# Raising the scheduler's priority of the attention row pairs in a hybrid FoX and mLSTM layer

## The chip, the cores and the metric

The kernel runs on one core of one Trainium2 chip. Its time is the device time of one execution in microseconds (us). The core has five engines that each work off their own queue of instructions in order: TensorE (PE, matrix products), VectorE (DVE), ScalarE (ACT), GpSimd (POOL) and SyncE (SP, which here issues DMAs). An instruction that needs something from another engine waits at the head of its queue, and what stands behind it waits too.

## The reference

One layer of a hybrid decoder: x is 2048 tokens of width 1024, in float32.

```
h  = rmsnorm(x);  z = h @ w_in                       # q, k, v, gates
fox = softmax(q k^T * d^-0.5 + c_t - c_s, causal) v  # 8 heads of 64, c = cumsum(log_sigmoid(f))
ml  = chunkwise matrix memory, 4 heads of 128
x  = x + concat(headnorm(fox), headnorm(ml) * sigmoid(o)) @ w_out
x  = x + relu(rmsnorm(x) @ w_up)^2 @ w_down
x  = x + sigmoid(rmsnorm(x) @ w_pg) * (p @ w_ple);  return rmsnorm(x)
```

The change touches only the order in which the `fox` line is worked.

## The kernel before

The program has three stretches. Up to about 560 us it makes the mLSTM half and the first projections. From about 560 to 1322 us it works the FoX attention. After that come the output projection, the MLP and the gate.

Attention goes head by head, and in a head by row pairs: `ROWS` pairs the sixteen blocks of 128 query rows as (15), (14, 0), (13, 1) to (8, 6), (7), so that nine steps have nearly the same work. A pair's scores lie side by side in *units*, tiles of 1024 columns; a head has 17 units, all heads 136. A name such as `s1_8_0_4` says head 1, the pair that begins with row block 8, the pair's first row block (0), key blocks from 4 on; `sp1_8_1`, `ph1_8_1` and `pt1_8_1` are unit 1 of that pair. Below, "unit 13,1 of head 1" means `..1_13_1`.

For each pair `fox_rows` records this chain:

- PE makes scores in chunks of at most 512 columns (L798, L800, for the diagonal also L803) into PSUM tiles `s`, of which there are three (SB).
- DVE adds the bias, keeps the running maximum and writes the unit's tile `sp` (L806); four `sp` tiles exist (SPB). Then DVE makes the exponent's offset `nb` (L818).
- ACT takes the exponential in place (L821), then casts the unit to float16 in a tile `ph` (L826); four `ph` tiles exist (PHB), and the norms borrow them too (`psq`, `po`).
- POOL, for each eighth unit DVE, subtracts the cast from the exact value for a second float16 half (L828).
- SP issues a DMA that transposes both halves into a tile `pt` (L830); three exist (PTB).

`fox_av` then multiplies the transposed unit with the values on PE (L846, L847, L849), three small matmuls a key block, and DVE copies the result out (L852). `fox_post` norms a group of finished rows and sends it on.

`fox_attn` calls these: a head begins with the loads of its two bias tiles (L890) and their scaling (L893); for each pair it records `fox_rows`, then a share of filler work (`fill`: the next heads' projections `zfq`, `zv`, `zfk`, the embedding product `pp`, the mLSTM output product `om`), and the value products of the pair that was recorded LAG = 3 pairs earlier.

What is recorded is not yet the order of the engines. The framework simulates a list scheduler: every instruction gets a priority by its place in the recording, and each engine takes, among the instructions whose inputs and buffers it holds to be ready by then, the one with the best priority. The result is a fixed queue for each engine; waits on semaphores are put in, and on the chip the order can't change any more. A tile taken again (the fifth `sp`, the fourth `pt`) waits there for the last use of the one that had its place.

Of the kernel before, what the change touches and what calls it, by code (L numbers as in the profile page):

```python
# [54 lines left out]
def hybrid_layer(ctx, tc, x, p, w_in, b_fox_f, b_mlstm_i, b_mlstm_f, w_conv, g_mix,  # L55
# [725 lines left out]
    def fox_rows(fl, fpp, h, rows, bias, fs, qkl):  # L781


        Qt, Kt, KL = qkl
        tag = f"{h}_{rows[0]}"
        nu = (sum(rows) + len(rows) + 7) // 8
        st = [fl.tile([P, 1024], F32, tag="sp", name=f"sp{tag}_{u}", bufs=SPB)
              for u in range(nu)]
        at = 0
        for r, i in enumerate(rows):  # L790
            qs = slice(i * P, (i + 1) * P)
            mx, kb, parts = None, 0, []
            while kb <= i:
                u, o = divmod(at + kb, 8)
                n = min(4, 8 - o, 8 - kb % 8, i + 1 - kb)
                ps = fpp.tile([P, 512], F32, tag="s", name=f"s{tag}_{r}_{kb}", bufs=SB)
                ks = slice(kb * P, (kb + n) * P)
                PE.matmul(ps[:, 0:n * P], lhsT=Qt[:, qs], rhs=Kt[:, ks], start=True, stop=False)  # L798
                diag = kb + n > i
                PE.matmul(ps[:, 0:n * P], lhsT=Qt[:, qs], rhs=KL[:, ks], start=False,  # L800
                          stop=not diag)
                if diag:
                    PE.matmul(ps[:, (n - 1) * P:n * P], lhsT=identb, rhs=fneg, start=False,  # L803
                              stop=True)
                m = fl.tile([P, 1], F32, tag="mx", name=f"mx{tag}_{r}_{kb}", bufs=8)
                V.tensor_tensor_reduce(out=st[u][:, o * P:(o + n) * P], in0=ps[:, 0:n * P],  # L806
                                       in1=bias[kb // 8][:, kb % 8 * P:(kb % 8 + n) * P],
                                       scale=1.0, scalar=-3.0e38 if mx is None else mx,
                                       op0=ALU.add, op1=ALU.max, accum_out=m)
                mx = m  # L810
                if parts and parts[-1][0] == u:
                    parts[-1][2] = o + n
                else:
                    parts.append([u, o, o + n])
                kb += n
            at += i + 1
            nb = fl.tile([P, 1], F32, tag="nb", name=f"nb{tag}_{r}", bufs=8)
            V.tensor_scalar(nb, mx, fs[:, 1:2], LN_P, op0=ALU.mult, op1=ALU.add)  # L818
            for u, o0, o1 in parts:
                sl_ = st[u][:, o0 * P:o1 * P]  # L820
                A.activation(sl_, sl_, AF.Exp, bias=nb, scale=fs[:, 0:1])  # L821
        pts = []
        for u in range(nu):
            ph = fl.tile([P, 2048], F16, tag="ph", name=f"ph{tag}_{u}", bufs=PHB)
            cnt[0] += 1
            A.copy(ph[:, 0:1024], st[u])  # L826
            eng = V if cnt[0] % DM == 3 else T
            eng.tensor_sub(ph[:, 1024:2048], st[u], ph[:, 0:1024])  # L828
            pt = fl.tile([P, 16, P], F16, tag="pt", name=f"pt{tag}_{u}", bufs=PTB)
            SP.dma_start_transpose(out=pt, in_=ph)  # L830
            pts.append(pt)
        return pts
# [23 lines left out]
    def drain(n):  # L856
        while sum(e[0] for e in avq) > n or (avq and not avq[0][0]):
            e = avq.pop(0)
            if e[0]:
                fox_av(*e[1:])  # L860
            else:
                posts.append([PD_, *e[1:]])

    def mix_load(lo, hi):

        for g in GD:
            if lo:
                mt_ = tp.tile([P, 2, KT, GT], F16, tag="T", name=f"mix{g}")
                mg[g] = mt_[:, 0], mt_[:, 1]
            gs = slice(g * GT, (g + 1) * GT)  # L870
            for a in range(2):
                SP.dma_start(out=mg[g][a][:, lo:hi, :],
                             in_=mixd[lo:hi, :, a, gs].rearrange("k p s -> p k s"))
                yield

    def late(all_=False):
        for e in posts:
            e[0] -= 1
        while posts and (all_ or posts[0][0] <= 0):
            fox_post(*posts.pop(0)[1:])  # L880

    def fox_attn(fl, fpp, j, z, fill):
        fs, iv, vt, qkls = z
        ogs = {}
        for hh in range(2):
            h = 2 * j + hh
            bias = {}
            for sg in (1, 0):
                b = fl.tile([P, 1024], F32, tag="bias", name=f"bias{h}_{sg}", bufs=2)
                SP.dma_start(out=b.rearrange("p (t s) -> p t s", s=P),  # L890
                             in_=crow[h * NT + 8 * sg:h * NT + 8 * sg + 8, :]
                             .partition_broadcast(P))
                V.tensor_scalar(b, b, fs[:, 2:3], None, op0=ALU.mult)  # L893
                bias[sg] = b
            for k, rows in enumerate(ROWS):
                pts = fox_rows(fl, fpp, h, rows, bias, fs, qkls[hh])
                for i in rows:
                    if hh == 0 and i // 4 not in ogs:
                        ogs[i // 4] = fl.tile([P, 4, 2, FD + 1], F32, tag="og",
                                              name=f"og{j}_{i // 4}", bufs=4)  # L900
                fill(sum(rows) + len(rows) + RC)
                avq.append((1, fl, fpp, h, rows, pts, vt, ogs))
                if hh == 1 and k in DONE:
                    g = DONE[k]
                    avq.append((0, fl, j, g, ogs[g], iv))
                drain(LAG)
                late()
                if h == FH - 2 and k == LK:
                    loads.append(mix_load(0, NP - 1))
                if loads:  # L910
                    next(loads[0], None)
        if j == NP - 1:
            for _ in loads[0]:
                pass
            for k in range(LAG - 1, -1, -1):
                fill(FE)
                drain(k)
                late()
            fill(1e9)
            late(all_=True)  # L920
# [36 lines left out]
    with phase("fl", 2) as fl, phase("fps", 2, PSUM) as fpp:  # L957
        def filler(parts, total):

            parts = iter(parts)  # L960
            st = [0.0, next(parts, None)]

            def fill(n):
                flush()
                st[0] += n * total / (272.0 + 18 * RC)
                while st[1] is not None and st[0] >= st[1]:
                    st[0] -= st[1]
                    st[1] = next(parts, None)
            return fill

        for j in range(NP):
            nxt = []
            if j < NP - 1:
                if j == 0:
                    plsp[0] = fl.tile([P, S], F16, name="plsp", bufs=1)
                    ple_w()
                fill = filler(pair_parts(j, nxt), TOT)
            else:
                for _ in mix_load(NP, KT):
                    pass  # L980
                fill = filler(late_parts(), FT)
            fox_attn(fl, fpp, j, box[0], fill)
            fill(1e9)
            second_keys()
            box = nxt
# [207 lines left out]
```

## Time and profile before

| | |
|---|---|
| median of three runs | 2950.56 us (2950.12 to 2952.53) |
| the profiled execution | 2954.44 us, of it 2952.7 us span |
| mean granted clock of TensorE | 0.968 of full speed |
| PE busy over the span | 2698.4 us (91%) |
| DVE, ACT, POOL busy | 1621.7, 1008.3, 698.7 us |
| attention, 560 to 1322 us | PE busy 608.1 of 762 us |
| after attention, 1322 to 2952.7 us | PE busy 1591.0 of 1630.7 us |

How to read it: time is lost where PE stands idle or is granted less than full clock. An engine's idle time has a releaser, the event that ended it; the views of waits add these up by the pair of lines. Busy shares over the whole span hide that nearly all of PE's idle time of the second half lies in attention.

### The profile page before, as it was taken

How to read it: one execution, taken by the hardware profiler on the slowest of the kernel's cores; microseconds unless marked ns; L12 is line 12 of the kernel's file. 1: busy time of each engine (PE TensorE's matmuls, PEld its weight loads, DVE VectorE, ACT ScalarE, POOL GpSimd, SP SyncE). 2: the span in 40 equal slices, each digit the busy share in tenths (PEclk: the TensorE clock that was granted, in tenths of full speed). 3: DMA queues.
4: the chain of work that ended last, by engine and by line, in shares of the span. 5: the costliest groups of instructions: out<-in, count | busy, mean ns of one | idle time of the engine just before them, and what ended most of it. 6: DMA issues, size and time to landing. Idle time of an engine off the chain costs nothing. (4 is left out here: it accounts for less than half of the span.)

```text
span 2952.7 us, 45034 instructions
## 1 busy us (share of the span) xinstructions
PE 2698.4 (91%) x18229; PEld 1507.1 (51%) x18229; DVE 1621.7 (55%) x3633; ACT 1008.3 (34%) x1686; POOL 698.7 (24%) x435
## 2 busy tenths in 40 slices
PE   4998999888878788788999999999999999999997
PEld 2756767555454554343344444444444444444686
DVE  6464654766757657556654444444444444445636
ACT  6244444465555555553411111111111111113532
POOL 1011110244343444343122111111212111111132
PEclk9999999989899989999999999999999999999999
DMA  9212220387686879996700000000000000002623
GB/s 243 45 44 59 58 47 20 94 167 137 139 166 133 165 169 219 196 205 222 148 29 29 29 29 16 28 15 29 29 29 29 29 29 16 28 15 43 143 69 136
DMA packets 535265, 256.36 MB, mean 87 GB/s; under 512 B 432784, under 2 KB 502672, under 8 KB 535056
## 3 DMA queue, kind: packets, MB, share of 16 engines
q1 hardware_dynamic: 525296, 236.66, 35.0%
q10 hardware_dynamic: 9760, 16.82, 1.8%
q8 instruction: 142, 2.33, 0.3%
q14 instruction: 67, 0.55, 0.1%
HBM read 113.88 MB, written 32.60 MB: 50 GB/s over the span
## 5 line engine op out<-in xcount | busy, mean ns | idle before, releaser
L1054 PE MATMUL d<-wd_hl,hid 128*128 128x512 f16 x3072 | 678.2, 380 | 8.4 <-DVE x L1059 8.2
L1036 PE MATMUL h<-y1t,wu_hl 128*128 128x512 f16 x3072 | 673.5, 379 | 0.5 <-issue 0.5
L1054 PEld LDWEIGHTS <-hid 128*128 128x128 f16 x3072 | 301.3, 98 | 375.0 <-issue 15.8
L1036 PEld LDWEIGHTS <-wu_hl 128*128 128x128 f16 x3072 | 300.5, 98 | 363.2 <-ACT y1y L200 1.0
L1059 DVE SCALAR_TENSOR_TENSOR x<-d,fac,x 128x512 f32<-128x512 f32 x512 | 373.8, 747 | 132.2 <-PE d L1054 131.8
L1044 POOL TENSOR_TENSOR hid<-r,hid 128x512 f16<-128x512 f32 x128 | 174.5, 1364 | 765.2 <-ACT hid L1043 659.1
L1042 DVE SCALAR_TENSOR_TENSOR r<-h,r 128x512 f32<-128x512 f32 x128 | 88.3, 690 | 458.2 <-ACT r L1040 458.1
L1040 ACT ACTIVATE r<-h 128x512 f32<-128x512 f32 x128 | 75.9, 594 | 766.8 <-PE h L1036 763.3
L828 POOL TENSOR_TENSOR ph<-sp,ph 128x1024 f16<-128x1024 f32 x119 | 255.9, 2164 | 283.3 <-ACT ph L826 219.3
L271 PEld LDWEIGHTS <-yt 128*128 128x128 f16 x3072 | 251.6, 101 | 40.1 <-issue 13.7
L260 PE MATMUL zqk<-yt,wqk_hl 128*128 128x512 f16 x768 | 188.7, 393 | 27.9 <-DMA yt<-yy 27.9
L821 ACT ACTIVATE sp<-sp,nb,fs 128x1024 f32<-128x1024 f32 (+3 forms) x192 | 177.9, 982 | 85.2 <-DVE nb L818 60.5
L798 PE MATMUL s<-K,Q 128*128 128x512 f16 (+3 forms) x320 | 117.9, 369 | 79.4 <-DVE mx L806 76.4
L846 PE MATMUL av<-vt,pt 128*128 128x65 f16 x1088 | 121.9, 199 | 67.3 <-DMA pt<-ph 55.6
L271 PE MATMUL zvo<-wvo_hl,yt 128*128 128x256 f16 x1536 | 175.0, 275 | 4.1 <-ACT wvo_hl L155 2.8
L1007 PE MATMUL pg<-wpg_hl,y2t 128*128 128x256 f16 x1536 | 171.0, 275 | 4.7 <-DVE x L1059 4.0
L1007 PEld LDWEIGHTS <-y2t 128*128 128x128 f16 x1536 | 151.6, 99 | 24.1 <-issue 5.1
L826 ACT CAST ph<-sp 128x1024 f16<-128x1024 f32 x136 | 137.8, 1038 | 67.9 <-DMA pt<-ph 62.6
L846 PEld LDWEIGHTS <-pt 128*128 128x128 f16 x1088 | 105.3, 100 | 75.1 <-DMA pt<-ph 67.8
L806 DVE CUSTOM_DVE_ANT_0 sp<-s,bias,mx 128x512 f32<-128x512 f32 (+2 forms) x192 | 124.5, 648 | 29.4 <-POOL ph L828 14.2
L260 PEld LDWEIGHTS <-wqk_hl 128*128 128x128 f16 x768 | 77.4, 101 | 105.5 <-ACT wqk_hl L155 25.9
L641 PEld LDWEIGHTS <-mix 128*128 128x128 f16 x768 | 76.4, 102 | 101.6 <-issue 27.7
(380 smaller groups left out, 3648.2 us busy)
## 6 DMA issues: line engine op xcount, KB each, us to landing
x<-in_x_dram SPq DMA_DIRECT2D x32, 512.0 KB, 5.8
wu_st<-in_w_up_dram SPq DMA_DIRECT2D x16, 1024.0 KB
wd_st<-in_w_down_dram SPq DMA_DIRECT2D x16, 1024.0 KB, 4.9
bias<-crow SPq DMA_DIRECT2D x16, 512.0 KB, 5.9
pled<-fox_st ACTq DMA_DIRECT2D x32, 256.0 KB, 2.8
wod<-spare ACTq DMA_DIRECT2D x32, 256.0 KB, 5.0
wos<-wod SPq DMA_DIRECT2D x32, 256.0 KB, 3.9
emb<-pled SPq DMA_DIRECT2D x32, 256.0 KB, 3.0
```

Of the source, the lines that this page charges most:

```text
L260: PE.matmul(ps, lhsT=hl[:, a, kt, m * P:(m + 1) * P], rhs=yT[g][b][:, kt, :], start=i == 0, stop=i == 3 * KT - 1)
L271: PE.matmul(ps[:, 0:n], lhsT=yT[g][b][:, kt, o:o + P], rhs=hl[:, a, kt, 0:n], start=i == 0, stop=i == 3 * KT - 1)
L806: V.tensor_tensor_reduce(out=st[u][:, o * P:(o + n) * P], in0=ps[:, 0:n * P], in1=bias[kb // 8][:, kb % 8 * P:(kb % 8 + n) * P], scale=1.0 ...
L821: A.activation(sl_, sl_, AF.Exp, bias=nb, scale=fs[:, 0:1])
L826: A.copy(ph[:, 0:1024], st[u])
L828: eng.tensor_sub(ph[:, 1024:2048], st[u], ph[:, 0:1024])
L846: PE.matmul(ar, lhsT=pt[:, o, :], rhs=vs[:, 0:65], start=kb == 0, stop=False)
L1007: PE.matmul(ps, lhsT=aT[t // 4][ya][:, kt, o:o + P], rhs=hl[:, wa, kt, :], start=i == 0, stop=i == 3 * KT - 1)
L1036: PE.matmul(ps, lhsT=wu[:, a, kt, m * P:(m + 1) * P], rhs=y1T[g][b][:, kt, :], start=i == 0, stop=i == 3 * KT - 1)
L1044: T.tensor_sub(hid[:, 1, m], r2, hid[:, 0, m])
L1054: PE.matmul(ps, lhsT=hid[:, a, m, t * P:(t + 1) * P], rhs=wd[:, b, m, hf * 512:(hf + 1) * 512], start=i == 0, stop=i == 5)
L1059: V.scalar_tensor_tensor(xs, ps, fac, xs, ALU.mult, ALU.add)
```

## The change

One call is put into a block that sets the scheduler's priority.

```
             for k, rows in enumerate(ROWS):
-                pts = fox_rows(fl, fpp, h, rows, bias, fs, qkls[hh])
+                with tc.high_priority():
+                    pts = fox_rows(fl, fpp, h, rows, bias, fs, qkls[hh])
                 for i in rows:
```

Within the block every instruction that `fox_rows` records, from the score matmul to the issue of the transpose, gets a priority ahead of all that is recorded outside: projections, value products, their copies, norms, bias loads. Each block starts its count at zero again, so that the instructions of two row pairs tie: the tenth of a later pair ranks with the tenth of an earlier one, not behind the earlier pair's last. No instruction is added, removed or changed; every buffer count is as before. After the changed line the line numbers of the new kernel are greater by one.

On PE, in head 1 near the end of its nine pairs, the rows below run from the last value product of unit 13,0 to the first score chunk of pair (7). First the kernel before:

```order
L849 MATMUL av_6239<-vt0_5167,pt1_13_0_7431 128x65
...
L798 MATMUL s1_9_0_0_7956<-K_5163,Q0_5162 128x512
...
L849 MATMUL av_6239<-vt0_5167,pt1_12_1_7606 128x65
L798 LDWEIGHTS Q0_5162
L798 MATMUL s1_8_0_0_8080<-K_5163,Q0_5162 128x512
...
L849 MATMUL av_6239<-vt0_5167,pt1_11_1_7750 128x65
L798 LDWEIGHTS Q0_5162
L798 MATMUL s1_7_0_0_8203<-K_5163,Q0_5162 128x512
```

The same stretch of the changed kernel:

```order
L798 MATMUL s1_8_1_0_8100<-K_5163,Q0_5162 128x512
...
L849 MATMUL av_6239<-vt0_5167,pt1_13_0_7431 128x65
...
L798 MATMUL s1_8_1_4_8105<-K_5163,Q0_5162 128x384
...
L260 MATMUL zfk1_2_8002<-yt2_285,fox_hl_5118 128x512
L798 LDWEIGHTS Q0_5162
L798 MATMUL s1_7_0_0_8203<-K_5163,Q0_5162 128x512
...
L798 MATMUL s2_15_0_0_8365<-K_5163,Q1_5944 128x512
...
L846 MATMUL av_6239<-vt0_5167,pt1_12_0_7601 128x65
```

Before, the value products of pairs (12, 2) and (11, 3), the scores of two pairs and 48 matmuls of `zfk` lie between the first row and `s1_7_0_0`. Now it is 24 value matmuls of unit 13,1, one score chunk and 21 matmuls of `zfk1_2`, and even the next head's first scores (`s2_15_0_0`) stand ahead of the value products of pair (12, 2).

On ACT, the exponentials (L821), casts (L826) and copies of keys (L769) of head 1 around pair (9, 5), before:

```order
L821 ACTIVATE sp1_10_1_7831<-sp1_10_1_7831,nb1_10_1_7863,fs0_5299 128x640
L826 CAST ph1_10_0_7866<-sp1_10_0_7830 128x1024
L769 ACTIVATE K_5163<-zfk1_1_7878 64x512
L826 CAST ph1_10_1_7871<-sp1_10_1_7831 128x1024
L821 ACTIVATE sp1_9_0_7954<-sp1_9_0_7954,nb1_9_0_7972,fs0_5299 128x1024
L821 ACTIVATE sp1_9_1_7955<-sp1_9_1_7955,nb1_9_0_7972,fs0_5299 128x256
```

and of the changed kernel:

```order
L826 CAST ph1_10_0_7866<-sp1_10_0_7830 128x1024
L769 ACTIVATE K_5163<-zfk1_1_7878 64x512
L821 ACTIVATE sp1_9_0_7954<-sp1_9_0_7954,nb1_9_0_7972,fs0_5299 128x1024
L821 ACTIVATE sp1_9_1_7955<-sp1_9_1_7955,nb1_9_0_7972,fs0_5299 128x256
L821 ACTIVATE sp1_9_1_7955<-sp1_9_1_7955,nb1_9_1_7987,fs0_5299 128x768
L826 CAST ph1_10_1_7871<-sp1_10_1_7831 128x1024
```

The cast of unit 10,1 now stands behind the three exponentials of the next pair.

On SP, the transposes (L830) and the loads of head 2's bias (L890) at the end of head 1, before:

```order
L830 DMA_TRANSPOSE pt1_10_0_7869<-ph1_10_0_7866 128x16x128
L890 DMA bias2_1_8357<-crow_382 128x1024
L830 DMA_TRANSPOSE pt1_10_1_7874<-ph1_10_1_7871 128x16x128
...
L830 DMA_TRANSPOSE pt1_7_0_8220<-ph1_7_0_8217 128x16x128
L716 DMA fox_st_5119<-in_w_in_dram 128x8x128
L890 DMA bias2_0_8360<-crow_382 128x1024
```

and of the changed kernel:

```order
L830 DMA_TRANSPOSE pt1_11_0_7745<-ph1_11_0_7742 128x16x128
L890 DMA bias2_1_8357<-crow_382 128x1024
L890 DMA bias2_0_8360<-crow_382 128x1024
L830 DMA_TRANSPOSE pt1_11_1_7750<-ph1_11_1_7747 128x16x128
L830 DMA_TRANSPOSE pt1_10_0_7869<-ph1_10_0_7866 128x16x128
```

The second bias load (`bias2_0`), which has to wait for the last use of head 1's `bias1_0` by pair (7), moves ahead of eight transposes.

## Rows read from the trace of the kernel before

**Rows 1.** Windows by stretch, columns named in the first line; PEclk is the granted clock.

```profile
core 0: us, PE busy (x) PEld busy (x) DVE busy (x) ACT busy (x) POOL busy (x), PEclk, DMA share, GB/s
560.00:1322.00 762.00, 608.10 (x6322) 369.70 (x6321) 489.55 (x1516) 414.99 (x530) 309.00 (x159) 0.92 0.80 163
680.00:768.00 88.00, 74.09 (x754) 42.67 (x751) 65.14 (x186) 43.15 (x56) 30.65 (x17) 0.96 0.70 133
768.00:874.00 106.00, 78.10 (x976) 55.78 (x974) 63.89 (x228) 57.25 (x79) 41.43 (x23) 0.92 0.79 155
1322.00:2952.70 1630.70, 1591.04 (x8085) 792.87 (x8081) 822.11 (x1353) 350.85 (x587) 327.55 (x233) 0.99 0.19 54
```

**Rows 2.** Waits of PE, 560 to 1322 us: line, releaser, total us, times, longest.

```profile
PE s L798 <- DVE mx L806: 76.4, 43, 4.9
PE av L846 <- DMA pt<-ph: 55.6, 35, 6.6
```

**Rows 3.** Waits of DVE, 560 to 1322 us.

```profile
DVE bias L893 <- DMA bias<-crow: 31.1, 12, 6.2
DVE sp L806 <- POOL ph L828: 27.8, 19, 5.9
```

**Rows 4.** Waits of ACT, 560 to 1322 us.

```profile
ACT ph L826 <- DMA pt<-ph: 62.6, 26, 6.0
```

**Rows 5.** Waits of SP's queue, 560 to 1322 us.

```profile
SPq L830 <- PE av L849: 53.1, 23, 5.9
```

**Rows 6.** Line L830, the transposes: issue min/median/max ns; then issue to landing.

```profile
L830 SPq DMA_TRANSPOSE pt<-ph x136: 1317/2472/7229, 584.4 to 1313.0; - x136
...
DMA to landing us min/median/max: 4.3/5.2/10.1
```

**Rows 7.** Timeline, PE, head 1: start, duration, line, operation, [idle before, its releaser].

```profile
706.99 0.19 PE L849 MATMUL av<-vt,pt 128*128 128x65 f16 x1
707.70 0.20 PE L847 MATMUL av<-vt,pt 128*128 128x64 f16 x1
710.12 0.38 PE L798 MATMUL s<-K,Q 128*128 128x512 f16 x1 [0.85 <-DVE mx L806]
711.30 4.70 PE L260 MATMUL zfk<-yt,fox_hl 128*128 128x512 f16 x21
```

**Rows 8.** Timeline of the same stretch, SP's queue, ACT, POOL and DVE.

```profile
707.26 14.58 SPq L830 DMA_TRANSPOSE pt<-ph  x4
711.75 1.04 ACT L826 CAST ph<-sp 128x1024 f16<-128x1024 f32 x1 [4.58 <-DMA pt<-ph]
712.92 2.14 POOL L828 TENSOR_TENSOR ph<-sp,ph 128x1024 f16<-128x1024 f32 x1 [3.98 <-DVE mx L806]
709.98 0.08 DVE L806 DVE_READ_ACCUMULATOR2_ANT mx<- 128x1 f32 x1
710.21 0.75 DVE L806 CUSTOM_DVE_ANT_0 sp<-s,bias,mx 128x512 f32<-128x512 f32 x1
```

**Rows 9.** Timeline, PE, the first chunks that wait in heads 2, 4 and 5.

```profile
753.47 0.39 PE L798 MATMUL s<-K,Q 128*128 128x512 f16 x1 [3.16 <-DVE mx L806]
754.34 0.63 PE L798 MATMUL s<-K,Q 128*128 128x512 f16 x1
939.16 0.39 PE L798 MATMUL s<-K,Q 128*128 128x512 f16 x1 [2.59 <-DVE mx L806]
1035.14 0.58 PE L798 MATMUL s<-K,Q 128*128 128x512 f16 x1 [4.32 <-DVE mx L806]
```

**Rows 10.** Timeline, DVE and SP, the end of head 1 and start of head 2.

```profile
732.40 0.73 DVE L806 CUSTOM_DVE_ANT_0 sp<-s,bias,mx 128x512 f32<-128x512 f32 x1
744.21 0.58 SPq L890 DMA_DIRECT2D bias<-crow  x1
750.96 0.75 DVE L893 TENSOR_SCALAR bias<-bias,fs 128x1024 f32<-128x1024 f32 x1 [1.31 <-DMA bias<-crow]
```

**Rows 11.** Window of PE behind the wait at 753.47: length, busy, granted clock, DMA share.

```profile
753.00:757.00 4.00, 3.53 (x11) 0.63 0.18 64
```

## The prediction

> **What bounds the kernel now.** I read the windows by stretch first. After attention PE is busy 1591.0 of 1630.7 us, and the change moves nothing there. In attention it is busy 608.1 of 762 [rows 1], so 153.9 us of idle time are all that the change can win, and new idle time there is all that it can lose. No other engine is full: DVE, the busiest after PE, has 490 of 762.
>
> The waits of PE come second. Two pairs of lines hold most of the 154 us: a score chunk that waits until DVE has read the chunk three before it (76.4 us in 43 waits), and a value product that waits for its transposed unit (55.6 us in 35) [rows 2]. The waits of DVE, ACT and SP say what stands behind the first: DVE waits 31.1 us for bias tiles and 27.8 us, in 19 waits, for POOL to leave an `sp` tile [rows 3]; ACT's cast waits 62.6 us for the transpose that frees a `ph` tile [rows 4]; SP's transposes wait 53.1 us for the value products that free a `pt` tile [rows 5].
>
> So there is a round trip through the tiles that are taken again. Counted in units, the transpose of unit u waits for the value products of u-3, the cast for the transpose of u-4, the score pass of DVE for the subtraction of u-4, and a score chunk for the DVE pass three chunks earlier. A score chunk so waits for value products eleven units back. The timeline gives its length. In head 1 the last value matmul of unit 13,0 ends at 706.99 + 0.19 = 707.18 [rows 7]; SP goes on at 707.26; the cast starts at 711.75, released by a landing; POOL's subtraction runs from 712.92 to 715.06 [rows 8]. That is 7.9 us. A DVE pass of 0.75 us follows, and about 0.14 us from the read of the maximum at 709.98 to the matmul it releases at 710.12 [rows 7, 8]: 8.8 us. For the second unit of a pair, whose value products end 24 x 0.031 = 0.75 us later (0.031 by the 23 steps from 706.99 to 707.70 [rows 7]), but whose transpose stands behind one of 2.47 us [rows 6], it is 8.8 + 2.47 - 0.75 = 10.5 us.
>
> **The change part by part.** It adds and removes no instruction, so PE's 608.1 us of attention stay, and the sum is made of waits. I count PE work between two instructions from the new order with three durations: 0.216 us for 512 columns (20 steps in 4.70 less the last one's 0.38 us), in proportion below that, and 0.031 us for a value matmul [rows 7].
>
> *The round trip: +27 us.* The order of before leaves it room: the distance on PE from the value products of u-11 to the chunk that waits for them is 8.9 us at least, 21.4 in the median, and one unit of 136 is short, by half a microsecond. After the change the median is nearly the same, 20.8, but a tenth of the units have 7.0 or less. The extract of PE's order shows one: from the last value matmul of unit 13,0 to `s1_7_0_0` there were 17.7 us of work, now 24 x 0.031 + 0.38 (the chunk `s1_8_1_4`) + 21 x 0.216 = 5.7 us, where 8.8 are needed. All in all 26 units are short, by 0.1 to 3.7 us each: 13 in head 1, three at the start of head 2, two at the end of head 3, three at the start of head 4, four at the end of head 5, one in head 7. Each alone they make 64 us, but a wait lengthens the windows that it lies in: counted along the order, with each wait added to the later windows that contain it, 33 us are left (19.5 around head 1, 6.8 about the border of heads 3 and 4, 6.8 in head 5). PE stops inside such windows for other reasons too, as for 0.85 us at 710.12 [rows 7]; for some thirteen windows that do not overlap I take 0.5 us off each, 6 us. Behind a waiting score chunk stand the projections and value products, which could have run: PE's queue does not let them by, as the 3.16 us at 753.47 show, with a ready `zfq` matmul right behind the chunk [rows 9].
>
> *The bias loads: -8 us.* Before, the loads for head 2 stand behind the last transposes of head 1. The pass of pair (7), which frees the tile, is over at 733.1; the load is issued at 744.21, and scaled at 750.96 [rows 10]. PE's fourth chunk of head 2 waits 3.16 us on that, and likewise 2.59 in head 4 and 4.32 in head 5 [rows 9]. In the new order these loads stand eight places earlier at the end of heads 1 and 3, which takes the first two away; in head 5 one place is won, and I take half: 3.16 + 2.59 + 2.2 = 8. The moved load adds a wait: it needs the DVE pass of pair (7), and the transpose of unit 11,1 is queued behind it. But that transpose needs a `pt` tile that the value products of 12,0 free, and these now stand behind the scores of pair (7) on PE. So it costs nothing beside that, or about the 0.6 us of an issue [rows 10] in each of three heads.
>
> *Casts behind exponentials, and the other waits: -2 us.* The cast of unit 10,1 stands behind three more exponentials, but before the change ACT waited 4.58 us at just this cast [rows 8], so they fit in. For value products the distance from those three units earlier falls short of 5.5 us 18 times instead of 25, 20 instead of 27 us in all; against that the chunks are recorded more tightly, and short of 2.5 us from one to the third after it by 129 in all instead of 121. The first says -6.5, the second +8.5, of which the 76.4 us measured against 121 counted make about half real: -2. I would not be surprised by -15 or +10.
>
> *Clock: 0.* After the 3.16 us idle at 753.47 the rows show matmuls of 0.63 us instead of 0.39 [rows 9] and a granted clock of 0.63 over 4 us [rows 11], about 1.5 us lost; after 2.59 us at 939.16 they don't. The waits that go and those that come stand against each other here.
>
> Sum: 2954.4 (the profiled execution) + 27 - 8 - 2 = 2971.4. The median of the runs lies 3.9 us below the profiled one, so I expect 2967.5, say 2968.
>
> **The rivals.** *Faster, about 2920.* Every chain from score to transpose starts earlier in heads 1 to 3 and 5, by 5 to 12 us of PE work. If the value products' wait for transposed units (55.6 us) falls by half and the bias waits go, and the round trip turns out no longer than 6 us because an early start fills the tiles ahead of need, the sum is -28 - 8, less 4: 2914 to 2925. For it speaks that PE's waits name late producers. The Trainium skill, "Perfetto Trace Analysis", Identifying Performance Opportunities, Optimization Strategy, says to find what blocks the gaps of the busiest engine and make these dependencies start sooner; by that rule the change wins. Against it: the long waits of value products lie in heads 2, 4, 6 and 7, where the order moves scores least.
>
> *No change, 2945 to 2956.* Four `sp`, four `ph` and three `pt` tiles limit how far scores can run ahead in either order; a wait that shows at the score chunk is then taken from the value product behind it, and the 27 us come out of the 55.6. For it: ACT, SP and DVE wait for tiles already [rows 3 to 5], and head 2 loses 28 of its 106 us, twice what head 1 does (14 of 88) [rows 1], where norms hold `ph` tiles in both orders. The same section of the Trainium skill says that a gap that repeats can mean too little buffer for the next tile; by it, no priority moves much.
>
> *Much slower, about 3010.* The waits do not shelter each other. PE stalls at each of the 26 units in full, since a stall delays the value products that start the next round trip: 64 - 10 = 54 us. It decides if the period of a pair in head 1 becomes the round trip rather than PE's work. Waits near 3 us then also take the clock down, 1.5 us each: 13 of them add 20 at most.
>
> *The other bound of what no row shows.* If SP's reordered bias load does hold up transposes by a full landing (5.2 us [rows 6]) in heads 0, 1 and 3, that adds 15 us to the forecast: 2983.
>
> **How the numbers follow.** Forecast, slower by some 10 to 35 us: 0.45. Much slower: 0.12. No change: 0.15. Faster: 0.28. A measurement of this kernel can tell 0.2%, 5.9 us, from no change; so slower holds 0.57, same 0.15, faster 0.28. The range: the forecast's own is 2957 to 2990; it must reach into the faster case and the much slower one until a tenth is left on each side: 2918 to 3010.
>
> **What would show it right or wrong.** Right: in the profile after, PE's wait of score chunks for DVE grows from 76 to about 95 to 105 us, DVE's wait for POOL from 28 to 50 or more, most of it in head 1 and at the ends of heads 3 and 5; head 1 grows from 88 to over 100 us; the 3.16 and 2.59 us at the first chunks of heads 2 and 4 are gone. The prediction is wrong if DVE's wait for POOL does not grow (the round trip is shorter or does not bind), or if it grows and the value products' wait for transposes falls by as much (the no-change case), or if heads 6 and 7, whose order hardly differs, hold most of the difference.

## The result, and the profile after

The changed kernel is slower: 2978.17 us (2972.76 to 2978.24) against 2951.55 us for the kernel before (2950.12 to 2955.93), a ratio of 1.0076 with a 95% interval of 1.0064 to 1.0087. (The quotient of the two medians is 1.0090, just above that interval.) A second series gave 1.0086 (1.0056 to 1.0115). Forecast were 2968 us, slower. Its profiled execution took 2972.76 us, 18.3 more than that of before; it is the fastest of its four, so the traces show two thirds of the difference of the medians, 26.6 us.

The windows of the changed kernel are cut where PE has done the same amount of work as at the borders of [rows 1], so they can be laid beside each other (the second is head 1):

```profile
560.00:1334.00 774.00, 613.54 (x6328) 366.50 (x6326) 475.27 (x1499) 419.69 (x532) 307.81 (x158) 0.93 0.77 160
683.00:779.00 96.00, 78.26 (x822) 45.88 (x819) 57.16 (x179) 45.17 (x58) 28.70 (x16) 0.93 0.64 129
1334.00:2970.70 1636.70, 1591.22 (x8088) 793.01 (x8088) 822.52 (x1364) 348.04 (x584) 324.83 (x233) 0.99 0.19 54
```

Attention takes 12 us more, the stretch after it 6 us more. Summed from 540 us to the last matmul of the output projection, the gaps ahead of PE's matmuls (those over 40 ns) are 162.6 us before and 178.1 after, +15.5; the time that isn't gap goes from 727.8 to 729.9, +2.1. The profile after was 2.3 us ahead when it reached attention (the first `zfk` starts at 537.02 instead of 539.29), so that ten matmuls of that projection fewer lie in its window. Counted from 540 us, at equal work, the delay grows in heads 0, 1, 3 and 5 (by 3.2, 7.6, 7.1 and 6.5 us), stays in head 2 and shrinks in heads 4 and 6 (by 5.4 and 7.1).

The waits of PE, from 560 to 1340 us, the same two lines as [rows 2] and what is new below them:

```profile
PE s L798 <- DVE mx L806: 78.7, 62, 4.1
PE av L846 <- DMA pt<-ph: 61.0, 47, 4.7
...
PE zfq L260 <- DVE fox_hl L156: 4.2, 1, 4.2
PE zfq L260 <- ACT fox_hl L155: 4.1, 2, 3.1
PE pp L609 <- DVE vt L763: 4.0, 1, 4.0
```

The waits of the other engines in the same stretch, first DVE, then ACT, then SP's queue, to be read beside [rows 3 to 5]:

```profile
DVE sp L806 <- POOL ph L828: 89.8, 47, 7.5
...
DVE bias L893 <- DMA bias<-crow: 19.9, 9, 5.1
```

```profile
ACT ph L826 <- DMA pt<-ph: 92.3, 42, 6.4
```

```profile
SPq L830 <- PE av L849: 69.9, 23, 9.5
```

The reader is to see two things that do not fit together at first. DVE's wait for POOL has tripled, from 27.8 to 89.8 us. Yet PE's wait of score chunks for DVE has grown only from 76.4 to 78.7, with shorter waits in more places. Where did 62 us of DVE's waiting go? The timeline of head 1 answers it. It is the place of [rows 7, 8] one pair on: the chunk `s1_7_0_0`, for which the prediction counted 5.7 us of work against 8.8 needed. PE first, with the last value matmul of unit 13,0 on top, then ACT and POOL, then DVE:

```profile
716.93 0.19 PE L849 MATMUL av<-vt,pt 128*128 128x65 f16 x1
718.95 5.52 PE L260 MATMUL zfk<-yt,fox_hl 128*128 128x512 f16 x21
725.34 0.38 PE L798 MATMUL s<-K,Q 128*128 128x512 f16 x1 [0.87 <-DVE mx L806]
```

```profile
721.59 1.04 ACT L826 CAST ph<-sp 128x1024 f16<-128x1024 f32 x1 [3.95 <-DMA pt<-ph]
722.77 2.13 POOL L828 TENSOR_TENSOR ph<-sp,ph 128x1024 f16<-128x1024 f32 x1 [7.05 <-ACT ph L826]
```

```profile
724.93 0.35 DVE L806 CUSTOM_DVE_ANT_0 sp<-s,bias,mx 128x128 f32<-128x128 f32 x1 [5.40 <-POOL ph L828]
```

From the end of the value matmul at 717.12 to the end of the subtraction at 724.90 there are 7.8 us, the round trip as forecast (7.9). DVE waits 5.40 us for it. But PE has 21 matmuls of `zfk` to do meanwhile, 5.52 us (4.70 for the same 21 before [rows 7]; the granted clock is 0.85 here and was 1.00 there), and the pass is a short one of 0.35 us; so of the 3.1 us counted only 0.87 show at the score chunk. A few microseconds on, DVE stands still again, and this time what stands behind in its queue matters. DVE and then PE:

```profile
738.44 0.69 DVE L806 CUSTOM_DVE_ANT_0 sp<-s,bias 128x512 f32<-128x512 f32 x1 [4.07 <-POOL ph L828]
739.05 0.08 DVE L806 DVE_READ_ACCUMULATOR2_ANT mx<- 128x1 f32 x1
739.05 2.91 DVE L156 TENSOR_TENSOR fox_hl<-fox_st,fox_hl 128x1024 f16<-128x1024 f32 x1
```

```profile
742.02 3.60 PE L260 MATMUL zfq<-yt,fox_hl 128*128 128x512 f16 x8 [4.22 <-DVE fox_hl L156]
```

The score pass at 738.44 waits 4.07 us for POOL; behind it in DVE's queue is L156, which finishes the weights of the next projection; PE waits 4.22 us for these. But L156 also needs the cast L155 of these weights, and that had stood behind a waiting cast in ACT's queue:

```profile
735.15 1.05 ACT L826 CAST ph<-sp 128x1024 f16<-128x1024 f32 x1 [3.01 <-DMA pt<-ph]
736.10 1.04 ACT L155 CAST fox_hl<-fox_st 128x1024 f16<-128x1024 f32 x1
```

L155 ends at 737.14 and L156 starts at 739.05, so at most 1.9 us of the delay arose in DVE's queue; the rest came through ACT's, where the cast L826 waited for a transpose. Both queues stood still for the same late score unit, and the wait for a score tile has come out at a projection.

Why does POOL release the tiles later? I followed each of these waits of DVE back in the trace: to the subtraction, to the cast before it, and, where that cast was released by a landing, to the transpose and what let it start. No view of the profile gives this table, and the border between its second and third row is a matter of how a wait with both causes is counted; their sum is not.

| DVE's wait for POOL at L806, us | before | changed |
|---|---|---|
| cast waited for a transpose that had just been let go by value products (the round trip) | 0 | 34.5 |
| cast waited for no landing: behind its own or a later pair's exponentials on ACT | 15.0 | 37.0 |
| cast done, subtraction queued on POOL | 12.8 | 17.2 |
| other | 0.2 | 1.6 |

The round trip holds up no score tile in the kernel before, and 34.5 us in the changed one: 13.9 in head 1, 4.1, 4.5, 5.1 and 6.9 in heads 2 to 5, none in 0, 6 and 7.

### The profile page after: what moved, and what is told of

Its sections match the earlier page's. It is cut to its first block, busy times and chain, and to the rows that moved or that the text cites. A ratio compares the mean times of both kernels' runs of the same rounds, so it can differ in the third digit from the quotient of the medians.

```text
span 2970.7 us, 44977 instructions
## 1 busy us (share of the span) xinstructions
PE 2700.1 (91%) x18229; PEld 1502.1 (51%) x18229; DVE 1610.8 (54%) x3633; ACT 1010.6 (34%) x1686; POOL 696.3 (23%) x435
## 3 DMA queue, kind: packets, MB, share of 16 engines
q1 hardware_dynamic: 525296, 236.66, 34.5%
## 5 line engine op out<-in xcount | busy, mean ns | idle before, releaser
L1055 PEld LDWEIGHTS <-hid 128*128 128x128 f16 x3072 | 301.3, 98 | 373.5 <-issue 13.7
L828 POOL TENSOR_TENSOR ph<-sp,ph 128x1024 f16<-128x1024 f32 x119 | 258.6, 2188 | 303.1 <-ACT ph L826 191.6
L260 PE MATMUL zqk<-yt,wqk_hl 128*128 128x512 f16 x768 | 185.2, 388 | 27.0 <-DMA yt<-yy 27.0
L821 ACT ACTIVATE sp<-sp,nb,fs 128x1024 f32<-128x1024 f32 (+3 forms) x192 | 178.3, 983 | 86.0 <-DVE nb L818 83.4
L798 PE MATMUL s<-K,Q 128*128 128x512 f16 (+3 forms) x320 | 117.9, 370 | 84.0 <-DVE mx L806 78.7
L826 ACT CAST ph<-sp 128x1024 f16<-128x1024 f32 x136 | 137.7, 1039 | 92.4 <-DMA pt<-ph 92.3
L806 DVE CUSTOM_DVE_ANT_0 sp<-s,bias,mx 128x512 f32<-128x512 f32 (+2 forms) x192 | 124.4, 648 | 58.0 <-POOL ph L828 43.9
L260 PEld LDWEIGHTS <-wqk_hl 128*128 128x128 f16 x768 | 76.6, 100 | 102.1 <-ACT wqk_hl L155 25.0
```

What stands on the lines that cost most here:

```text
L260: PE.matmul(ps, lhsT=hl[:, a, kt, m * P:(m + 1) * P], rhs=yT[g][b][:, kt, :], start=i == 0, stop=i == 3 * KT - 1)
L1055: PE.matmul(ps, lhsT=hid[:, a, m, t * P:(t + 1) * P], rhs=wd[:, b, m, hf * 512:(hf + 1) * 512], start=i == 0, stop=i == 5)
```

## The experiments

Each series ran beside the kernel before on the same chip; ratios are against it, with their 95% intervals. In the code below, the lines under an added `with` line stand inside its block. Three theories stood against each other. **Round trip**: scores placed too close behind the value products that free their tiles. **Fillers**: projections and norms, pushed behind every row pair, come too late. **Ties**: since each block counts from zero, later pairs' exponentials stand ahead of earlier casts and transposes.

**Even heads alone.**

```
-                with tc.high_priority():
+                with (tc.high_priority() if hh == 0 else ExitStack()):
```

> The priority block is kept for the even heads alone (0, 2, 4, 6). Round trip (score chunks placed closer than 8.8 to 10.5 us behind the value products that free their tiles): in this order no unit of 136 is short (26 in the changed kernel), so the time falls back to that of the kernel before or below, 2940 to 2956 us, and DVE's wait for POOL at L806 to 25 to 45 us. Rival, fillers: everything outside the row pairs is pushed back and each pair under priority pays its share, so half the pairs pay half of 26 us: about 2965. Rival, ties (later pairs' scores ahead of earlier pairs' transposes): also about half, 2965.

2964.34 us, 1.0033 (1.0023 to 1.0043). Slower than forecast by the round trip, by some 8 us, and as the rivals had it. But the round trip itself is gone, as forecast: DVE's wait for POOL is 41.1 us, and of it 0.1 goes back to value products. What is left is PE's wait for transposed units, 71.7 us against 55.6 before, in heads 2 and 4. So there is a second cost that has nothing to do with the round trip. It is not small: PE's gaps add up to 180.0 us in this profile, as many as in the changed kernel.

```profile
DVE sp L806 <- POOL ph L828: 41.1, 28, 8.2
```

```profile
PE s L798 <- DVE mx L806: 73.1, 50, 5.6
PE av L846 <- DMA pt<-ph: 71.7, 37, 7.5
```

**Odd heads alone** (the same line with `hh == 1`).

> The priority block is kept for the odd heads alone (1, 3, 5, 7). Round trip: 20 units are short, 34 us counted along the order, as much as the 33 of the changed kernel, so 2970 to 2990 us, and DVE waits 70 to 100 us for POOL at L806. Rivals, fillers and ties: half of the 26 us, about 2965, the same as the even heads alone.

2990.97 us, 1.0123 (1.0102 to 1.0143): as the round trip had it, one us above its range, and 26 us above the even heads, where the rivals had the two the same; so neither fillers nor ties alone can be the cause. Half of the edit costs more than the whole of it. DVE's wait for POOL is 92.4 us, 37.3 of it from value products, and here it shows at the score chunks:

```profile
DVE sp L806 <- POOL ph L828: 92.4, 42, 7.6
```

```profile
PE s L798 <- DVE mx L806: 108.4, 58, 8.0
PE av L846 <- DMA pt<-ph: 54.0, 36, 5.5
```

**No ties.**

```
-                with tc.high_priority():
+                with tc.high_priority(offset=4000):
```

> The changed kernel with high_priority(offset=4000): the row pairs still outrank all that is outside, but keep their order among themselves. Round trip: 30 units are short, 45 us along the order against 33, and value products stand more tightly behind those three units earlier (50 us short of 5.5 against 20), so slower than the changed kernel: 2985 to 3005 us. Rival, ties: the later pairs' exponentials no longer stand ahead of earlier casts and transposes, so most of the 26 us comes back: 2950 to 2962.

2991.05 us, 1.0120 (1.0102 to 1.0137). The ties alone are not the cause: without them the kernel is slower still. They do have a part: the waits behind casts without a landing fall from 37.0 to 21.2 us; 28.9 go back to value products, less than in the changed kernel (34.5), though 45 against 33 were counted. It is slower for what the order adds at other places, as at the projections (PE waits 5.4, 5.4, 4.8 and 3.4 us there).

**The front of a row pair alone** (score matmuls to exponentials, the first line added below), and **the back alone** (cast, subtraction and transpose, the second), each on the kernel before:

```
+        with tc.high_priority():
         at = 0
         for r, i in enumerate(rows):
...
+            with tc.high_priority():
             ph = fl.tile([P, 2048], F16, tag="ph", name=f"ph{tag}_{u}", bufs=PHB)
...
             SP.dma_start_transpose(out=pt, in_=ph)
```

> The priority block holds only the front of a row pair: scores, DVE passes, nb and exponentials. Casts, subtractions and transposes stand outside it. Round trip: 17 units are short, 25 us along the order (changed kernel 26 and 33), in heads 1 and 5, so 2965 to 2985 us, with DVE's wait for POOL at L806 above 55 us. Rival: what costs time is that casts and transposes go ahead of projections and norms on ACT and SP; then this order is like the kernel before, 2946 to 2958.

> The priority block holds only the back of a row pair: cast, subtraction, transpose. Scores and exponentials stand outside it. Round trip: no unit is short, so 2946 to 2960 us, DVE's wait for POOL at L806 20 to 40 us. Rival (casts and transposes ahead of projections and norms): most of the 26 us, 2968 to 2980.

The front alone: 2978.49 us, 1.0076 (1.0051 to 1.0102), as much as the whole edit, with 61.0 us of DVE's wait for POOL, 21.9 of them from value products (25 were counted). Its profiled execution is the fastest of six, 2958.56 us, 20 us below the median. The back alone: 2946.89 us, 0.9970 (0.9956 to 0.9984), a little faster than before, 47.1 us and none from value products. What costs time is that the scores and exponentials move ahead, not that casts and transposes do.

**The bias loads alone**, on the kernel before, and **together with the back**:

```
             for sg in (1, 0):
+                with tc.high_priority():
                 b = fl.tile([P, 1024], F32, tag="bias", name=f"bias{h}_{sg}", bufs=2)
                 SP.dma_start(out=b.rearrange("p (t s) -> p t s", s=P),
...
                 V.tensor_scalar(b, b, fs[:, 2:3], None, op0=ALU.mult)
```

> The kernel before, with the priority block around the bias loads and their scaling (L890, L893) instead of the row pairs. My term of 8 us: no unit is short of the round trip, the waits of the first chunks of heads 2, 4, 5, 6 and 7 for the bias (some 19 us together) shrink, so 2935 to 2947 us. Rival: a bias that comes earlier uncovers the next wait (DVE's norms, transposes), or its wait on SP holds up transposes: 2948 to 2956.

> Priority for the back of a row pair (cast, subtraction, transpose) and for the bias loads with their scaling; scores outside. Round trip: no unit is short, the distances from one score chunk to the third after it fall short of 2.5 us by 109 us in all (121 in the kernel before, 112 with the bias loads alone), so as fast as the bias loads alone or a little faster: 2934 to 2946 us, below both kernels. Rival: the two edits get in each other's way on SP, 2946 to 2956.

The bias loads: 2943.11 us, 0.9965 (0.9949 to 0.9980), the size forecast, but not for the reason. DVE's wait for the bias falls from 32.5 to 13.7 us (540 to 1360 us), yet the gaps of PE add up to 162.2 us, as before (162.6): score chunks wait 91.9 us instead of 76.4, value products 42.4 instead of 55.6. What falls is the time in which PE is busy, from 727.7 to 719.5 us. The windows from 540 us to the end of the output projection, before and with the bias loads moved:

```profile
540.00:1430.70 890.70, 727.70 (x6863) 423.04 (x6862) 583.51 (x1718) 465.22 (x624) 342.51 (x183) 0.93 0.80 170
540.00:1421.90 881.90, 719.47 (x6850) 416.54 (x6849) 598.63 (x1713) 465.67 (x624) 344.98 (x182) 0.93 0.80 171
```

The granted clock is 0.93 in both. Among the matmuls of 512 columns, 30 fewer of the projections take over 0.5 us instead of 0.38 (74 against 104), but 27 more of the scores do (73 against 46). PE was busy at the lower clock for 102.0 us instead of 107.8, which at half speed is worth about 3 us (an estimate). Another 2.7 us had been won ahead of attention (the first `zfk` starts at 536.57 instead of 539.29). Where the rest comes from stays open; that the bias waits gave the gain is not shown. Both together: 2940.32 us, 0.9956 (0.9940 to 0.9972), the lowest median here and below both kernels, but by its interval not told apart from the bias loads alone.

**The bias loads in the changed kernel.**

```
             for sg in (1, 0):
+                with tc.high_priority():
...
                 with tc.high_priority():
                     pts = fox_rows(fl, fpp, h, rows, bias, fs, qkls[hh])
```

> The changed kernel with the bias loads and their scaling in the priority block as well. Round trip: with the bias there sooner the scores are placed earlier still, 34 units are short and 43 us along the order (26 and 33 in the changed kernel), so the 10 us that the bias loads alone gave are lost again: 2972 to 2990 us. Rival, the terms simply add (row pairs +26, bias -11): 2964 to 2970.

2976.61 us, 1.0084 (1.0058 to 1.0109), against 1.0086 for the changed kernel beside it. The 10 us that the loads gave alone are gone from the median; DVE's wait for POOL is 121.5 us. By the median the terms do not add; the lower end of the interval, 2967 us, still lies in the rival's range.

**The value products too.**

```
-                drain(LAG)
+                with tc.high_priority():
+                    drain(LAG)
```

> The changed kernel with the value products and the copies of their results in the priority block too, so that they tie with the scores; projections, norms and bias loads stay behind both. Round trip: no unit is short, so DVE's wait for POOL at L806 falls from 90 to 25 to 45 us; but value products stand more tightly behind those three units earlier (52 us short of 5.5 in all, against 20), so PE's wait for transposed units grows from 61 to 75 us or more: 2955 to 2975 us. Rival, fillers: projections are pushed back further than in the changed kernel, so 2980 or more, with PE's waits at projections (L260, L609) above 13 us.

2982.32 us, 1.0094 (1.0076 to 1.0112): slower than I forecast. What was to go has gone: DVE's wait for POOL is 49.5 us, none from value products, and score chunks wait less than in any other kernel here. But value products now wait 98.1 us for their transposes, where I had 75 or more. At projections PE waits 2.8 us at L260 and 4.5 at `om`, so the rival's 13 us are not there. The mechanism is as I had it, the size is wrong; the time lies in the rival's range, without the rival's waits:

```profile
PE av L846 <- DMA pt<-ph: 98.1, 72, 5.7
PE s L798 <- DVE mx L806: 51.3, 49, 4.3
```

**A longer round trip in the kernel before.** The subtraction is followed by a second one of half the width that writes the same values again:

```
             eng.tensor_sub(ph[:, 1024:2048], st[u], ph[:, 0:1024])
+            eng.tensor_sub(ph[:, 1024:1536], st[u][:, 0:512], ph[:, 0:512])
```

> The kernel before with half of each subtraction done twice (512 more columns, about 1.1 us on POOL, 0.75 on DVE for each eighth unit), so that every round trip is about 1.1 us longer. Round trip: this order leaves it 8.9 us at least and 21 in the median, and no unit of the new order is short of the 9.9 us then needed, so hardly anything: 2951 to 2964 us. Rival, the chain from score to transpose itself sets the pace (PE's waits for transposed units): 1.1 us for each of the 72 pairs, 80 us, or half of that where it lies beside other waits: 2990 to 3030.

3008.25 us, 1.0187 (1.0158 to 1.0216). My forecast was far off, and the rival's range holds it. The added instruction takes 1.16 us on POOL in the median:

```profile
DVE sp L806 <- POOL ph L829: 69.3, 26, 12.1
```

```profile
PE s L798 <- DVE mx L806: 98.6, 51, 6.7
PE av L847 <- DMA pt<-ph: 59.6, 40, 5.3
```

But it isn't the rival's mechanism either: PE's wait for transposed units hardly moves (55.6 to 59.6 us), the wait for score tiles does (76.4 to 98.6). There is a shorter loop through POOL than mine, one without value products: a tile `sp` is filled, its maximum found, its exponential taken, cast and subtracted, and only then is it free for the unit four later. The table above had shown it: all 28 us of DVE's waiting in the kernel before are of that kind. I took their small sum for slack. Whether the latency of the subtraction or POOL's busy time (461.7 of 835 us here, 309 of 762 before [rows 1]) weighs more is open.

**The changed kernel once more.**

> The changed kernel once more, unaltered, for a second profile: the first profiled execution took 2972.8 us, the other three runs 2978.2. Round trip: idle time of PE behind 540 us about 15 to 20 us above that of the kernel before, as in the first profile, and DVE's wait for POOL at L806 75 to 100 us; the 5.4 us between its runs come from matmuls at a lower granted clock, not from other waits. Rival: the 5.4 us are one more wait.

2976.45 us (2970.45 to 2986.12), profiled at 2970.45. Gaps are 175.6 us, +13.0 on before, a little below the range; DVE waits 86.2 us for POOL, 34.7 of it from value products; time that isn't gap 733.4. The two profiles agree on these waits. What makes up the 5.4 us between its runs stays open, since again the fastest was the one profiled.

The order's count of short units, made before any of these ran, against what the traces show of the round trip, and PE's gaps from 540 us to the end of the output projection:

| kernel | units short, us along the order | DVE's waits from value products, us | all DVE waits for POOL, us | PE's gaps, us | ratio |
|---|---|---|---|---|---|
| before | 1, 0.5 | 0 | 27.8 | 162.6 | 1 |
| changed | 26, 33 | 34.5 | 89.8 | 178.1 | 1.0076 |
| odd heads | 20, 34 | 37.3 | 92.4 | 198.9 | 1.0123 |
| no ties | 30, 45 | 28.9 | 75.0 | 190.1 | 1.0120 |
| front | 17, 25 | 21.9 | 61.0 | 180.3 | 1.0076 |
| changed, bias | 34, 43 | 34.5 | 121.5 | 181.7 | 1.0084 |
| even heads | 0, 0 | 0.1 | 41.1 | 180.0 | 1.0033 |
| value products too | 0, 0 | 0 | 49.5 | 191.6 | 1.0094 |
| back | 0, 0 | 0 | 47.1 | 158.1 | 0.9970 |
| bias | 0, 0 | 0 | 27.7 | 162.2 | 0.9965 |
| back, bias | 0, 0 | 0 | 36.6 | 157.7 | 0.9956 |

The waits from value products appear in all five orders with 17 or more short units, and in none of the six with one or none (0.1 us of the even heads apart). The time follows them in part only: even heads and value products too are slow without them, and their gaps are as long as those of the changed kernel or longer, through value products that wait for transposes. So the round trip is shown on DVE, and that the scores' move ahead costs the time is shown by front and back; what share of the 15.5 us of gaps the round trip alone has is not shown. No run had more `sp`, `ph` or `pt` tiles, which would have loosened the round trip without moving any work.

## Why the prediction was right, and where it wasn't

**The direction and the net size: right.** The terms summed to +17 us; the profiled executions differ by 18.3, of which 15.5 are gaps. The medians differ by 26.6, and what makes up the other 8 us is in no trace. That the sum came so close is in part luck: the even heads alone have as many gaps without any round trip.

**Round trip, +27 us: the mechanism is shown on DVE, its way to PE was not as I put it.** The trip takes 7.8 us where I had 7.9. DVE's waits that go back to value products are 34.5 us where 33 were counted along the order, and stand where they were counted (13.9, 4.1, 4.5, 5.1 and 6.9 us in heads 1 to 5, against 16.3, 3.2, 3.2, 3.6 and 6.8). Odd against even heads and front against back tell it from the rivals. The step that failed is the equation of DVE's wait with PE's: DVE's wait for POOL grew past the 50 us that I had named, but at score chunks I expected 95 to 105 us and there are 78.7. Cutting each wait of PE at a score chunk by what DVE did meanwhile, passes and waits for POOL account for 34.6 us before and 51.6 after, +17; the waits at projections and for copies of keys (zfq, pp, L773) add some 10 more. Not all of that is the round trip: the waits behind casts without a landing are in it too. The rest of the score chunks' wait, DVE's other work, falls by some 15 us, which is why their total hardly moves. The prediction named what stands behind the waiting chunk on PE, and not what stands behind the waiting pass on DVE and the waiting cast on ACT: L156, L155 and the copies that projections wait for.

**Bias loads, -8 us: right at the score chunks.** The waits at the fourth chunks of heads 2, 4 and 5 (3.16, 2.59 and 4.32 us [rows 9]) are all gone, and over all score chunks' waits the time in which DVE waits for the bias or scales it falls from 13.4 to 3.0 us. Yet PE waits 4.22 us at `zfq` in head 2 and 3.14 in head 4, a moment earlier; these two are counted with the round trip above. Whether the 8 us would show as time is open, since the bias loads alone left the gaps as they were. The fear of transposes held up behind the early load was rightly priced low: in head 1 SP's two loads are through at 729.32 (725.32 + 4.00) and the transposes go on at once, when the value products of unit 12,0 have only just ended:

```profile
725.32 4.00 SPq L890 DMA_DIRECT2D bias<-crow  x2
729.44 11.93 SPq L830 DMA_TRANSPOSE pt<-ph  x4
```

**Casts behind exponentials, -2 us with the rest: wrong.** I reasoned that the exponentials fit into ACT's wait at one cast. Over all heads DVE's waits that go back to casts which waited for no landing grow from 15.0 to 37.0 us, and without ties they are 21.2. On DVE this is a second cause, two thirds as large as the round trip (22.0 us more against 34.5). And the value products' wait for transposes, for which I had -6.5 from the order's distances, rose by 5.4 us (55.6 to 61.0; but 54.6 in the second profile, so two profiles of one kernel differ by more), while that for the copies of results fell by 5.7 (11.6 to 5.9).

**Clock, 0: none to speak of.** PE was busy at the lower clock for 107.8 us before and 101.7 after. The time that isn't gap grows by 2.1 us, or by some 4 at equal work, and not through the clock. That gaps stand for the time held here; for the bias loads alone they explain none of the gain.

**Where: half right.** Heads 1, 3 and 5 lose, as forecast, but head 1 takes 96 us and not over 100, heads 4 and 6 give time back, and 6 us are lost behind attention, where I had nothing. There PE waits some 5 us more, in the output projection (8.6 us before) and at the MLP's first matmul (0.5 before):

```profile
PE o L641 <- DVE x L1097: 8.6, 2, 6.0
```

```profile
PE o L641 <- DVE x L1098: 10.7, 3, 6.3
PE h L1037 <- ACT y1y L200: 2.3, 1, 2.3
PE o L641 <- DMA mix<-po: 1.2, 1, 1.2
```

The first line is of the kernel before, the others of the changed one, 540 to 1480 us.

**The rivals.** Faster by an earlier start: the Trainium skill, "Perfetto Trace Analysis", Identifying Performance Opportunities, Optimization Strategy, says to find what blocks execution at the gaps of the busiest engine and to make it start sooner or complete faster. In this case that went with a gain where the back of a pair and the bias loads were put ahead (0.9956), though for the loads the gaps do not show why. For the scores it failed, as the front alone shows (1.0076). No change, by tiles that limit both orders: the same section says that a gap that repeats on the engine that should be full can mean too little room for the next tile. That engine is PE; behind its waits for scores DVE and ACT wait longest for tiles to come free (89.8 and 92.3 us), which agrees, but no run had more tiles. Much slower, by waits that do not shelter each other: the odd heads come nearest, with +36 us of gaps.

## What to carry to other kernels

A higher priority for the producer of a chain moves work ahead, but where the tiles of the chain are not yet free it only puts the waiting instruction at the head of a queue that is worked in order, and the price is what stands behind it there (4.22 us at a projection for one late score unit). Count the distance, in the order, between the instruction that frees a tile and the one that takes it again, and compare it with the latency of that loop in the trace; do so for every loop through the tile, the short one without the last consumer too. And try priority for what frees tiles before what fills them: here casts, subtractions and transposes ahead gave 0.9970 and scores ahead 1.0076. It is no rule: value products free tiles too, and put ahead beside the scores they gained nothing (1.0094).

## What the runs showed that I had not expected

A kernel can gain 10 us without a gap less: with the bias loads moved PE's gaps add up to the same 162 us at the same granted clock of 0.93, and a good part of the gain is unexplained. Between executions of one kernel the granted clock can weigh as much as such a change: of the six of the front alone, one at 0.977 took 2958.56 us, the other five, at 0.967 to 0.971, 2976.72 to 2983.12. Half an edit (odd heads, 1.0123) can cost more than the whole (1.0076). And 1.16 us more on POOL (the median) for each of 119 units, and 0.69 on DVE for 17, cost the kernel before 58 us, though POOL had been busy for only 309 of 762 us.
